# Up-projection of a gated MLP: half of the block moves go from GpSimd to ScalarE, one step behind the transposes, and the silu is issued behind the next evacuation

## The chip, the cores and the metric

The kernel runs on one core of one Trainium2 chip. The metric is the device time of one execution in microseconds. Five engines of the core work side by side, each through its own list of instructions in order: TensorE (PE in the profile; its weight loads are PEld), VectorE (DVE), ScalarE (ACT), GpSimd (POOL) and SyncE (SP), which here issues the loads of the weights. They wait for one another only through semaphores. Before the change three runs took 2243.81 to 2244.72 us, with a median of 2244.45 us.

## The reference

The program is a two-layer encoder over 256 positions of width 2048, in float32. Each layer has attention and then a gated MLP; the change lies in the MLP, which is, cut to what matters (D_FF is 5632):

```python
def conv_ffn(h, w_up, conv_w, conv_b, w_down):
    u = h @ w_up                                  # 256 x 11264: gates, then values
    u = lax.conv_general_dilated(u, conv_w[:, None, :], window_strides=(1,), padding=((1, 1),),
                                 feature_group_count=c) + conv_b   # width 3, along the positions
    gate, val = jnp.split(u, 2, axis=-1)
    return (jax.nn.silu(gate) * val) @ w_down
```

The convolution runs along the positions, channel by channel, so the kernel needs the channels on the partitions after the up-projection, which delivers positions on the partitions. Hence transposes stand between the two.

## The kernel before

**Products.** Every weight arrives as float32 in tiles `raw` of 128x1024 (512 KB). ScalarE rounds such a tile to `wh` (line 144) and VectorE takes the rest, `wl = raw - wh` (line 145). Each weight tile then feeds three passes of TensorE, `xh*wh`, `xh*wl` and `xl*wh` (lines 132 to 134), for two halves of the positions and two rows of weight blocks: twelve products of 128x512. There are four buffers each of `wh` and `wl` (`NHL`), so ScalarE can round a tile only when TensorE has finished with the one four before. In pairs 2, 4, 6 and 8 (`UP`) one of the four quarters of the inner dimension is done in Strassen's way (`fast_unit`, lines 179 and 180), where seven weight tiles feed six products each, and sums of weights and of results go over VectorE.

**The stages of the MLP.** The 5632 channels are 11 pairs of blocks of 512, a gate block and a value block each, in two halves (`HALVES`: pairs 0 to 5, then 6 to 10); after each half the down-projection runs over what is finished. In the profile the up-projections lie at about 290 to 550 and 670 to 850 us (layer 0) and 1550 to 1800 and 1905 to 2150 us (layer 1).

**A block behind the product.** For a gate (`gate_gen`) and a value (`value_gen`):

- ScalarE evacuates two accumulators to `stg` and applies the row scale (`evac_scaled`, line 489, two instructions).
- `turned` lets VectorE transpose 32x32 blocks into `quad` (line 377, two instructions), and then 16 moves of 32 partitions x 256 elements put the blocks in place in `u`. All 16 are GpSimd's (line 562), except for the value of the last pair of a half, where every second one is ScalarE's (line 564).
- `conv` runs the middle tap and the bias on ScalarE (line 541, four instructions) and the two outer taps on VectorE (line 549, eight instructions), into `cg` for a gate and `cv` for a value.
- The gate gets its silu on ScalarE (line 571), in the generator of the next pair's gate; `product` multiplies it with the value on VectorE (line 579); `act_split` or `combined` splits the result for the down-projection.

There are three `u` buffers, used in turn, two `quad`, one `cg` and one `cv`.

**What sets the order.** The generators are advanced by `step`, once for some products of the main line: every `yield` puts what follows one step later in the program. A scheduler then orders each engine's list by priority and dependence; the splits to `wh` and `wl` are pulled 60 places ahead (`tc.high_priority(offset=AHEAD)`), and `tc.issue_after(x)` keeps an instruction behind `x`. What stands in an engine's list is executed in that order, so an instruction that waits holds up all those behind it on its engine.

Of the kernel before, what the change touches and what calls it, by code (L numbers as in the profile page):

```python
# [10 lines left out]
AF = mybir.ActivationFunctionType  # L11
# [14 lines left out]
UP = 2, 4, 6, 8  # L26
UP_ORDER = (1, 0), (2, 0), (3, 0), (0, None), (1, 1), (2, 1), (3, 1)
NWARM = 11
QC = [(q, c) for q in range(4) for c in range(4)]
# [4 lines left out]
def tile_encoder(ctx: ExitStack, tc: tile.TileContext, x, xT, w_a, w_ao, q_gain, k_gain, w_b, w_bo,  # L34
                 rel_bias, gains, w_up, conv, w_down, final_norm, rope, ident_c, onehot, out):
    nc = tc.nc
# [23 lines left out]
    def nm(s):  # L60
        uid[0] += 1
        return f"{s}_{uid[0]}"
# [43 lines left out]
            return pool.tile([P, 2, 512], F32, tag=tags[0], name=nm("raw"), bufs=2 if len(tags) == 1 else 1)  # L106
        return spool.tile([P, 2, 512], F32, tag="raw", name=nm("raw"), bufs=NRAW)

    newest = [None]

    def of_m(x, m):
        return x[m] if isinstance(x, tuple) else x[:, m * P:(m + 1) * P]
# [41 lines left out]
    def new_acc():  # L154
        return [accp.tile([P, 512], F32, tag="acc", name=nm("acc")) for _ in range(2)]
# [214 lines left out]
    def quad_tile(pool, tag, bufs=1):  # L370
        return pool.tile([P, 4, 8, 32], F32, tag=tag, name=nm("quad"), bufs=bufs)
# [4 lines left out]
    def quad_T(quad, at, src):  # L376
        nc.vector.transpose(quad[:, :, at, :], src.rearrange("p (x c t) -> p c x t", c=4, t=32))  # L377
# [73 lines left out]
    def finish_rstd(ss):  # L451
        tot = small.tile([P, 2], F32, tag="tot", name=nm("tot"))
        nc.vector.tensor_reduce(tot, ss, axis=AX.X, op=ALU.add)
        rstd = small.tile([P, 2], F32, tag="rstd", name=nm("rstd"))
        rsqrt_mean(rstd, tot, D)
        return rstd
# [29 lines left out]
    def evac_scaled(pool, accs, rstd, bufs=2):  # L486
        o = pool.tile([P, 2, 512], F32, tag="stg", name=nm("stg"), bufs=bufs)
        for m in range(2):
            nc.scalar.activation(o[:, m, :], accs[m], AF.Copy, scale=rstd[:, m:m + 1])  # L489
        return o  # L490

    def ffn(l, hT, ss_in, cw, g_next, last, side=None):
        with tc.tile_pool(name=nm("fpool"), bufs=1) as fp:
# [7 lines left out]
            rstd = finish_rstd(ss_in)  # L501
# [4 lines left out]
            def fin(c0, c1):  # L506
                return fins[c0 // 512][:, c0 % 512:(c1 - 1) % 512 + 1]
# [43 lines left out]
                    if j == 1:  # L551
                        yield

            def turned(s, u, by_act=False):
                quad = quad_tile(fp, "quad", 2)
                for m in range(2):
                    quad_T(quad, slice(m, 8, 2), s[:, m])
                for i, (q, c) in enumerate(QC):
                    o = u[32 * c:32 * c + 32, :, :, 32 * q:32 * q + 32]
                    src = quad[32 * q:32 * q + 32, c].rearrange("p (j m) t -> p j m t", m=2)  # L560
                    if i % 2 == 0 or not by_act:
                        nc.gpsimd.tensor_copy(o, src)  # L562
                    else:
                        nc.scalar.activation(o, src, AF.Copy)

            def gate_gen(accs, blk, value):
                s = evac_scaled(fp, accs, rstd, 1)
                yield
                turned(s, blk[1])
                if value is not None:  # L570
                    nc.scalar.activation(value[3], value[3], AF.Silu)
                    for _ in range(4 if blk[0] in UP else 2 if blk[0] == 1 else 1):
                        yield
                    yield from product(value)

            def product(value):
                n, u, cv, cg, _, _ = value
                yield from conv((n, u, cv))
                nc.vector.tensor_tensor(cv, cg, cv, ALU.mult)

            def value_gen(accs, blk, gate, last):
                s = evac_scaled(fp, accs, rstd, 1)
                yield
                if gate[0] + 1 in (p for _, p in HALVES):
                    turned(s, blk[1], True)
                    yield
                    yield from conv(gate)
                    nc.scalar.activation(gate[2], gate[2], AF.Silu)
                    yield
                    yield from act_split(last)  # L590
                    return
                turned(s, blk[1])
                wait = 4 if gate[0] in UP else 5 if last is None else 2
                if last is not None:
                    yield
                    for _ in act_split(last):
                        yield
                        wait -= 1
                    wait -= 1
                for _ in range(max(wait, 1)):  # L600
                    yield
                yield from conv(gate)
# [53 lines left out]
            def next_u():  # L656
                us.append(us.pop(0))
                return us[0]
# [70 lines left out]
            for hf, (p0, p1) in enumerate(HALVES):  # L729
# [5 lines left out]
                for p in range(p0, p1):  # L735
# [3 lines left out]
                    gate, value = (p, next_u(), cg), (NPAIR + p, next_u(), cv, cg, slots, k0)  # L739
# [56 lines left out]
                def put(m, c0, c1, how, r):  # L796
                    hs = h[:, m, c0:c1]
                    if how == "fin":
                        nc.vector.scalar_tensor_tensor(hs, hs, r, fin(c0, c1), ALU.mult, ALU.mult)
                    elif how == "act":  # L800
                        nc.scalar.activation(hs, hs, AF.Copy, scale=r)
                    else:
                        nc.vector.tensor_scalar(hs, hs, r, None, op0=ALU.mult)
# [52 lines left out]
                accs = new_acc()  # L856
# [684 lines left out]
```

## Time and profile before

| | |
|---|---|
| median of three runs | 2244.45 us |
| the profiled execution, its own time | 2244.87 us |
| its span, from the first to the last instruction | 2243.1 us |
| mean granted TensorE clock | 0.999 |
| TensorE busy | 2218.4 us (99% of the span) |
| VectorE busy | 1885.2 us (84%) |
| ScalarE busy | 1344.4 us (60%) |
| GpSimd busy | 762.8 us (34%) |

The table of the costliest groups has one row for each line, engine and shape, with the total, the mean of one instruction in ns, the idle time of the engine just before them and what ended it. Its rows on matmuls read 390 ns for one, but they start every 0.227 us: consecutive matmuls overlap. So a time for TensorE has to be read from the starts, in the timeline, or from its idle stretches, in the view of the waits. A wait in that view reads "engine, line that waited <- engine and line that ended the wait: us in total, times, longest".

### The profile page before, as it was taken

Reading aid. Unit: us, or ns where it says so; the run is one execution under the profiler, and the core shown is the slowest. Engines: PE = TensorE matmul, PEld = TensorE weight load, DVE = VectorE, ACT = ScalarE, POOL = GpSimd, SP = SyncE. Lnnn points to the kernel's source line nnn. Section 1 sums busy time; section 2 is a strip of 40 time slices with the busy share of each in tenths; the row PEclk is TensorE's granted clock in tenths of the full one; section 3 lists DMA queues with packets and bytes.
Section 4 is the critical chain, followed back from the end, with each engine's and each line's share of the span. In section 5 each row is a group of like instructions: output and inputs, shape, how many; then the busy total and the mean of one; then the engine's idle time right before and its main releaser. Section 6 shows DMA issues by size and latency. Waiting matters only on the chain.

```text
span 2243.1 us, 28885 instructions
## 1 busy us (share of the span) xinstructions
PE 2218.4 (99%) x9957; PEld 1833.9 (82%) x9957; DVE 1885.2 (84%) x2385; ACT 1344.4 (60%) x1894; POOL 762.8 (34%) x1017
## 2 busy tenths in 40 slices
PE   9999999999999999999999999999999999999998
PEld 7888888788888878888888888888887888887887
DVE  6877678998898998868886878588899898989887
ACT  7666655666455666665454556566666655556664
POOL 2343254753006462040053006003645600255611
PEclk9999999999999999999999999999999999999999
DMA  8575655556656566666656555656556565656654
GB/s 302 192 215 182 218 186 194 183 192 196 203 183 226 175 198 202 197 188 197 188 186 197 179 189 181 195 185 214 174 197 201 185 203 191 215 162 205 226 196 142
DMA packets 126179, 439.59 MB, mean 196 GB/s; under 512 B 14408, under 2 KB 18248, under 8 KB 126032
## 3 DMA queue, kind: packets, MB, share of 16 engines
q1 hardware_dynamic: 123056, 429.05, 58.8%
q0 software_dynamic: 2688, 8.39, 1.5%
q8 instruction: 78, 1.28, 0.2%
q14 instruction: 69, 0.57, 0.1%
q10 hardware_dynamic: 288, 0.30, 0.0%
HBM read 432.34 MB, written 5.34 MB: 195 GB/s over the span
## 4 chain that ended last, share of the span: by engine, by line
PE 42%; DVE 8%; issue 2%; DMA 2%; POOL 1%; ACT 1%; DVEq 0%; POOLq 0%; ACTq 0%
PE acc L133 12%; PE acc L132 12%; PE acc L134 12%; DVE wl L145 3%; DVE wl L180 1%; DVE cv L549 1%; PE ps L187 1%; PE ps L188 1%; PE ps L186 1%; DMA raw<-in_w_b_dram 1%; POOL u L562 1%; DMA raw<-in_w_up_dram 1%; ACT wh L144 1%; DMA raw<-in_w_down_dram 1%; DVE cg L549 1%
## 5 line engine op out<-in xcount | busy, mean ns | idle before, releaser
L145 DVE TENSOR_TENSOR wl<-raw,wh 128x1024 fp32r<-128x1024 f32 (+1 forms) x716 | 898.8, 1266 | 224.2 <-ACT wh L144 218.3
L144 ACT ACTIVATE wh<-raw 128x1024 fp32r<-128x1024 f32 (+1 forms) x716 | 746.0, 1048 | 516.2 <-PE acc L134 391.9
L133 PE MATMUL acc<-wl,xh 128*128 128x512 f32 x2048 | 801.1, 391 | 8.7 <-DVE wl L145 8.7
L132 PE MATMUL acc<-wh,xh 128*128 128x512 f32 x2048 | 800.3, 391 | 1.3 <-ACT wh L144 1.3
L134 PE MATMUL acc<-wh,xh 128*128 128x512 f32 x2048 | 798.3, 390 | 0.0
L562 POOL COPY u<-quad 32x256 f32<-32x256 f32 x672 | 518.3, 771 | 451.1 <-DVE quad L377 414.1
L133 PEld LDWEIGHTS acc<-wl,xh 128*128 128x128 f32 x2048 | 385.2, 188 | 94.6 <-DVE wl L145 17.0
L132 PEld LDWEIGHTS acc<-wh,xh 128*128 128x128 f32 x2048 | 385.2, 188 | 80.8 <-ACT wh L144 2.4
L134 PEld LDWEIGHTS acc<-wh,xh 128*128 128x128 f32 x2048 | 385.0, 188 | 79.4
L132 PE MATMUL acc<-wh,a 128*128 128x512 f32 x720 | 281.1, 390 | 0.0
L133 PE MATMUL acc<-wl,a 128*128 128x512 f32 x720 | 280.7, 390 | 0.0
L134 PE MATMUL acc<-wh,a 128*128 128x512 f32 x720 | 280.3, 389 | 0.0
L179 ACT ACTIVATE wh<-raw 128x1024 fp32r<-128x1024 f32 x112 | 118.7, 1061 | 107.9 <-PE acc L134 82.9
L134 PEld LDWEIGHTS acc<-wh,a 128*128 128x128 f32 x720 | 135.2, 188 | 28.2 <-DVE a L328 0.2
L133 PEld LDWEIGHTS acc<-wl,a 128*128 128x128 f32 x720 | 135.3, 188 | 28.0 <-DVE wl L145 0.6
L132 PEld LDWEIGHTS acc<-wh,a 128*128 128x128 f32 x720 | 135.3, 188 | 27.5
L381 POOL COPY wide<-quad 32x256 f32<-32x256 f32 x133 | 89.3, 672 | 169.3 <-DVE quad L377 159.8
L180 DVE TENSOR_TENSOR wl<-raw,wh 128x1024 fp32r<-128x1024 f32 x112 | 137.2, 1250 | 1.6 <-ACT wh L179 1.0
L398 POOL COPY wide<-quad 32x256 f32<-32x256 f32 x88 | 53.2, 605 | 235.4 <-DVE quad L377 168.3
L489 ACT ACTIVATE stg<-acc,rstd 128x512 f32<-128x512 f32 x122 | 81.5, 682 | 33.5 <-PE acc L134 17.0
L549 DVE SCALAR_TENSOR_TENSOR cg<-u,cw,cg 128x256 f32<-128x256 f32 x176 | 94.3, 581 | 3.4 <-ACT cg L541 3.3
L549 DVE SCALAR_TENSOR_TENSOR cv<-u,cw,cv 128x256 f32<-128x256 f32 x176 | 85.8, 524 | 2.5 <-ACT cv L541 1.9
(310 smaller groups left out, 2198.6 us busy)
## 6 DMA issues: line engine op xcount, KB each, us to landing
raw<-in_w_up_dram SPq DMA_DIRECT2D x352, 512.0 KB, 4.5
raw<-in_w_down_dram SPq DMA_DIRECT2D x176, 512.0 KB, 4.6
raw<-in_w_b_dram SPq DMA_DIRECT2D x144, 512.0 KB, 4.5
raw<-in_w_bo_dram SPq DMA_DIRECT2D x48, 512.0 KB, 4.4
raw<-in_w_a_dram SPq DMA_DIRECT2D x40, 512.0 KB, 4.8
raw<-in_w_ao_dram SPq DMA_DIRECT2D x32, 512.0 KB, 4.6
raw<-in_w_a_dram SPq DMA_DIRECT2D x16, 256.0 KB, 5.8
there<-quad POOLq DMA_DIRECT2D x6, 512.0 KB, 3.7
```

The source lines that it names most:

```text
L132: nc.tensor.matmul(accs[m], xh, wh[:, j, :], start=st, stop=False)
L133: nc.tensor.matmul(accs[m], xh, wl[:, j, :], start=False, stop=False)
L134: nc.tensor.matmul(accs[m], xl, wh[:, j, :], start=False, stop=sp)
L144: nc.scalar.activation(wh[:, c], r[:, c], AF.Copy)
L145: newest[0] = nc.vector.tensor_tensor(wl[:, c], r[:, c], wh[:, c].bitcast(F32), ALU.subtract)
L179: nc.scalar.activation(wh, r, AF.Copy)
L180: nc.vector.tensor_tensor(wl, r, wh.bitcast(F32), ALU.subtract)
L381: nc.gpsimd.tensor_copy(o[32 * c:32 * c + 32, :, 32 * q:32 * q + 32], quad[32 * q:32 * q + 32, c])
L398: nc.gpsimd.tensor_copy(dst, src)
L489: nc.scalar.activation(o[:, m, :], accs[m], AF.Copy, scale=rstd[:, m:m + 1])
L549: nc.vector.scalar_tensor_tensor(cj, halves(flat[:, j, o:o + NT])[:, ::-1], tap(n, j, i), cj, ALU.mult, ALU.add)
L562: nc.gpsimd.tensor_copy(o, src)
```

## The change

`turned` becomes a generator. GpSimd makes the moves with even numbers, for every gate and every value. Then, unless `at_once` is set, it yields, and ScalarE makes the eight others one step later. The value of the last pair of a half passes `at_once` and is as before. The silu is put behind the newest evacuation (`evac[0]`). Some counts of steps are one smaller, since `turned` now takes a step itself.

```diff
-    newest = [None]
+    newest, evac = [None], [None]
...
-            nc.scalar.activation(o[:, m, :], accs[m], AF.Copy, scale=rstd[:, m:m + 1])
+            evac[0] = nc.scalar.activation(o[:, m, :], accs[m], AF.Copy, scale=rstd[:, m:m + 1])
...
-            def turned(s, u, by_act=False):
+            def turned(s, u, at_once=False):
                 quad = quad_tile(fp, "quad", 2)
                 for m in range(2):
                     quad_T(quad, slice(m, 8, 2), s[:, m])
-                for i, (q, c) in enumerate(QC):
-                    o = u[32 * c:32 * c + 32, :, :, 32 * q:32 * q + 32]
-                    src = quad[32 * q:32 * q + 32, c].rearrange("p (j m) t -> p j m t", m=2)
-                    if i % 2 == 0 or not by_act:
-                        nc.gpsimd.tensor_copy(o, src)
-                    else:
-                        nc.scalar.activation(o, src, AF.Copy)
+
+                def move(i, put):
+                    q, c = QC[i]
+                    put(u[32 * c:32 * c + 32, :, :, 32 * q:32 * q + 32],
+                        quad[32 * q:32 * q + 32, c].rearrange("p (j m) t -> p j m t", m=2))
+
+                for i in range(0, 16, 2):
+                    move(i, nc.gpsimd.tensor_copy)
+                if not at_once:
+                    yield
+                for i in range(1, 16, 2):
+                    move(i, partial(nc.scalar.activation, func=AF.Copy))
...
-                turned(s, blk[1])
+                yield from turned(s, blk[1])
                 if value is not None:
-                    nc.scalar.activation(value[3], value[3], AF.Silu)
-                    for _ in range(4 if blk[0] in UP else 2 if blk[0] == 1 else 1):
+                    with tc.issue_after(evac[0].ins):
+                        nc.scalar.activation(value[3], value[3], AF.Silu)
+                    for _ in range(3 if blk[0] in UP else 1):
                         yield
                     yield from product(value)
...
                 if gate[0] + 1 in (p for _, p in HALVES):
-                    turned(s, blk[1], True)
+                    yield from turned(s, blk[1], True)
...
-                turned(s, blk[1])
+                yield from turned(s, blk[1])
                 wait = 4 if gate[0] in UP else 5 if last is None else 2
                 if last is not None:
-                    yield
                     for _ in act_split(last):
```

The lists of TensorE and SyncE hold the same instructions in the same order as before; GpSimd's list has 320 moves fewer, ScalarE's 320 more; VectorE's has the same instructions, some in another order. Line 562 becomes 561, the silu's line 571 becomes 577, and other lines below move by five or six.

The first place is ScalarE's list in pair 2 of layer 0, after the evacuation of that pair's value. `cg<-u` is the middle tap of the pair's gate, `s` and `sx` are splits of the value of the pair before, `u_2635` is where this value's blocks go. Before:

```order
L489 ACTIVATE stg_3770<-acc_3362,rstd_2629 128x512
L144 ACTIVATE wh_3891<-raw_3887 128x1024
L541 ACTIVATE cg_3357<-u_2637,cw_555 128x256 x2
L144 ACTIVATE wh_3909<-raw_3889 128x1024
L541 ACTIVATE cg_3357<-u_2637,cw_555 128x256 x2
L320 ACTIVATE s_3842<-st_3837 128x1024
L320 ACTIVATE sx_3844<-cv_2994 128x512
L320 ACTIVATE sx_3844<-cv_2994 128x256
L144 ACTIVATE wh_3935<-raw_3931 128x1024
```

Now:

```order
L489 ACTIVATE stg_3770<-acc_3362,rstd_2629 128x512
L144 ACTIVATE wh_3891<-raw_3887 128x1024
L541 ACTIVATE cg_3357<-u_2637,cw_555 128x256 x2
L561 ACTIVATE u_2635<-quad_3802 32x8x32 x2
L144 ACTIVATE wh_3909<-raw_3889 128x1024
L561 ACTIVATE u_2635<-quad_3802 32x8x32 x6
L144 ACTIVATE wh_3935<-raw_3931 128x1024
L320 ACTIVATE s_3842<-st_3837 128x1024
L320 ACTIVATE sx_3844<-cv_2994 128x512
L320 ACTIVATE sx_3844<-cv_2994 128x256
L144 ACTIVATE wh_3955<-raw_3933 128x1024
L541 ACTIVATE cg_3357<-u_2637,cw_555 128x256 x2
```

Eight moves came in around `wh_3909`, and `wh_3935` now stands ahead of the three splits and of two of the four taps.

The second place is VectorE's list in pair 8 of layer 0, ahead of and behind `wl_7168`. `cv_6325` is the value of the pair before, first under its outer taps, then multiplied with its gate; the two rows on `acc` are the last sums of this pair's result. Before:

```order
L145 TENSOR_TENSOR wl_7131<-raw_7088,wh_7130 128x1024
L549 SCALAR_TENSOR_TENSOR cv_6325<-u_5965,cw_555,cv_6325 128x256 x3
L579 TENSOR_TENSOR cv_6325<-cg_6324,cv_6325 128x1024
L723 TENSOR_TENSOR acc_6692<-acc_6692,fold_6930 128x512
L724 TENSOR_TENSOR acc_6693<-acc_6693,fold_6930 128x512
L145 TENSOR_TENSOR wl_7168<-raw_7163,wh_7167 128x1024
L145 TENSOR_TENSOR wl_7184<-raw_7165,wh_7183 128x1024
L377 STREAM_TRANSPOSE quad_7111<-stg_7079 128x16x32 x2
```

Now:

```order
L145 TENSOR_TENSOR wl_7123<-raw_7088,wh_7122 128x1024
L549 SCALAR_TENSOR_TENSOR cv_6325<-u_5965,cw_555,cv_6325 128x256 x3
L145 TENSOR_TENSOR wl_7168<-raw_7163,wh_7167 128x1024
L728 TENSOR_TENSOR acc_6692<-acc_6692,fold_6930 128x512
L729 TENSOR_TENSOR acc_6693<-acc_6693,fold_6930 128x512
L549 SCALAR_TENSOR_TENSOR cv_6325<-u_5965,cw_555,cv_6325 128x256
L145 TENSOR_TENSOR wl_7184<-raw_7165,wh_7183 128x1024
L585 TENSOR_TENSOR cv_6325<-cg_6324,cv_6325 128x1024
L377 STREAM_TRANSPOSE quad_7111<-stg_7079 128x16x32 x2
```

`wl_7168` has moved ahead of the product and the two sums.

The third place is ScalarE's list in pair 8 of layer 0, behind the evacuation of its value, where the silu of its gate `cg_6688` stands. Before it was followed by the taps of the value, with `wh` in between:

```order
L144 ACTIVATE wh_7328<-raw_7290 128x1024
L571 ACTIVATE cg_6688<-cg_6688 128x1024
L541 ACTIVATE cv_6689<-u_5964,cw_555 128x256 x2
L144 ACTIVATE wh_7350<-raw_7346 128x1024
L541 ACTIVATE cv_6689<-u_5964,cw_555 128x256 x2
L489 ACTIVATE stg_7283<-acc_7084,rstd_2629 128x512
L489 ACTIVATE stg_7283<-acc_7085,rstd_2629 128x512
L144 ACTIVATE wh_7372<-raw_7348 128x1024
```

Now:

```order
L541 ACTIVATE cv_6689<-u_5964,cw_555 128x256 x2
L489 ACTIVATE stg_7283<-acc_7084,rstd_2629 128x512
L489 ACTIVATE stg_7283<-acc_7085,rstd_2629 128x512
L144 ACTIVATE wh_7366<-raw_7346 128x1024
L577 ACTIVATE cg_6688<-cg_6688 128x1024
L561 ACTIVATE u_5965<-quad_7308 32x8x32
L144 ACTIVATE wh_7392<-raw_7388 128x1024
L561 ACTIVATE u_5965<-quad_7308 32x8x32 x6
L144 ACTIVATE wh_7413<-raw_7390 128x1024
L561 ACTIVATE u_5965<-quad_7308 32x8x32
L541 ACTIVATE cv_6689<-u_5964,cw_555 128x256 x2
```

The silu moved behind the evacuation of the next gate (`stg_7283`), and that gate's moves stand right behind it.

## The prediction, made before the result was seen

> **What bounds the kernel now.** I read the busy times first, then the windows of the four up-projection stretches, then TensorE's own waits there, and last the timeline around the longest of them. The busy times, and the windows of those stretches (columns: length, then busy time and count of PE, PEld, DVE, ACT and POOL):
>
> ```profile
> PE 2218.4 (99%) x9957; PEld 1833.9 (82%) x9957; DVE 1885.2 (84%) x2385; ACT 1344.4 (60%) x1894; POOL 762.8 (34%) x1017
> ...
> 290.00:550.00 260.00, 256.45 (x1128) 210.96 (x1128) 234.69 (x286) 162.16 (x213) 145.77 (x185) 1.00 0.59 190
> 670.00:850.00 180.00, 178.20 (x782) 146.10 (x781) 162.10 (x197) 109.66 (x138) 102.82 (x132) 1.00 0.62 202
> 1550.00:1800.00 250.00, 248.15 (x1090) 203.66 (x1089) 226.91 (x277) 158.17 (x206) 141.07 (x184) 1.00 0.59 193
> 1905.00:2150.00 245.00, 242.94 (x1067) 199.45 (x1066) 218.49 (x267) 149.02 (x192) 118.05 (x156) 1.00 0.61 200
> sum 935.00, PE 925.74 PEld 760.16 DVE 842.18 ACT 579.01 POOL 507.70; mean PE 231.43 PEld 190.04 DVE 210.55 ACT 144.75 POOL 126.93
> ```
>
> TensorE bounds it, at full clock (the 1.00). Its products are untouched, so what can be won is only its stalls in these stretches: 935.0 - 925.7 = 9.3 us of idle time. VectorE stands next at 842/935 = 90%, ScalarE at 62%, GpSimd at 54%. TensorE's waits in the whole program, and one stall start by start (columns: start, us, instruction, idle before it):
>
> ```profile
> PE acc L133 <- DVE wl L145: 8.7, 11, 2.3
> PE ps L187 <- DVE wl L180: 2.0, 2, 1.2
> PE acc L132 <- ACT wh L144: 1.3, 2, 0.8
> ...
> 796.33 0.39 PE L134 MATMUL acc<-wh,xh 128*128 128x512 f32 x1
> 796.56 0.39 PE L132 MATMUL acc<-wh,xh 128*128 128x512 f32 x1
> 798.23 0.50 PE L133 MATMUL acc<-wl,xh 128*128 128x512 f32 x1 [1.29 <-DVE wl L145]
> 798.57 0.39 PE L134 MATMUL acc<-wh,xh 128*128 128x512 f32 x1
> ...
> 999.73 0.39 PE L134 MATMUL acc<-wh,xh 128*128 128x512 f32 x1
> 1007.89 0.39 PE L134 MATMUL acc<-wh,xh 128*128 128x512 f32 x1
> ```
>
> It almost always waits for `wl`, so for VectorE, seldom for `wh`. Between the last two rows lie 36 starts without a stall: 8.16/36 = 0.227 us each. Here the gaps are 1.67 and 0.34: 1.44 + 0.11 = 1.55 us lost for 1.29 of idle time, so 0.26 more for each stall. The stalls in the stretches are about nine (9.3 us at about 1 us each): 9.3 + 9 x 0.26 = 11.7 us is all that this change can recover there.
>
> **What makes VectorE late, and what half the moves buy.**
>
> ```profile
> L562 POOL COPY u<-quad 32x256 f32<-32x256 f32 x672 | 518.3, 771 | 451.1 <-DVE quad L377 414.1
> L549 DVE SCALAR_TENSOR_TENSOR cg<-u,cw,cg 128x256 f32<-128x256 f32 x176 | 94.3, 581 | 3.4 <-ACT cg L541 3.3
> L549 DVE SCALAR_TENSOR_TENSOR cv<-u,cw,cv 128x256 f32<-128x256 f32 x176 | 85.8, 524 | 2.5 <-ACT cv L541 1.9
> ...
> L549 DVE SCALAR_TENSOR_TENSOR cg<-u,cw,cg x176: 443/611/617, 310.5 to 2132.6; 128x256 f32<-128x256 f32 x176
> ...
> L145 DVE TENSOR_TENSOR wl<-raw,wh 128x1024 fp32r<-128x1024 f32 x38 | 46.5, 1223 | 7.8 <-ACT wh L144 7.2
> ...
> L145 DVE TENSOR_TENSOR wl<-raw,wh 128x1024 fp32r<-128x1024 f32 x4 | 5.4, 1355 | 0.0
> L723 DVE TENSOR_TENSOR acc<-acc,fold 128x512 f32<-128x512 f32 x1 | 0.7, 680 | 0.0
> ...
> L145 DVE TENSOR_TENSOR wl<-raw,wh 128x1024 fp32r<-128x1024 f32 x82 | 106.1, 1307 | 21.9 <-ACT wh L144 21.9
> L145 DVE TENSOR_TENSOR wl<-raw,wh 128x1024 fp32r<-128x1024 f32 x59 | 77.3, 1325 | 16.9 <-ACT wh L144 16.8
> L145 DVE TENSOR_TENSOR wl<-raw,wh 128x1024 fp32r<-128x1024 f32 x81 | 106.0, 1324 | 19.8 <-ACT wh L144 19.7
> L145 DVE TENSOR_TENSOR wl<-raw,wh 128x1024 fp32r<-128x1024 f32 x81 | 104.7, 1306 | 24.0 <-ACT wh L144 23.8
> ...
> L562 POOL COPY u<-quad x672: 391/480/2955, 298.8 to 2135.5; 32x256 f32<-32x256 f32 x168
> ```
>
> The first `wl` row is from a stretch of attention (1234 to 1342 us) without GpSimd work, the second from 786 to 798 us, where GpSimd moves blocks without a break; the last four are the up-projections of the two halves of layer 0 and of layer 1; rows with three numbers give min/median/max of one. With moves beside it an outer tap takes 0.611 instead of 0.443 us and a `wl` 1.355 instead of 1.223, while the sum that reads an accumulator takes 0.68. Over all taps that is 94.3 + 85.8 - 352 x 0.443 = 24.2 us; the 303 `wl` of the stretches took 394.1 - 303 x 1.223 = 23.5 us too long. 320 of 672 moves leave GpSimd, 48%: about 0.48 x 48 = 23 us of VectorE's time come back, 2.5% of the stretches. That the moves left on GpSimd get faster too is not counted.
>
> The Trainium skill explains these rows (SBUF — State Buffer, "Who interferes with whom"): a VectorE instruction with two SBUF inputs and a GpSimd instruction that reads SBUF exclude each other on a shared port for a whole instruction, and ScalarE never waits. The trace agrees in kind (two-input taps and `wl` stretch, 0.611 and 1.355 us, the accumulator sum does not), but not in a full exclusion of each other. Taken at its word each of the 320 moves would have held the port for its undisturbed 0.39 us (the shortest in the last row), an estimated 125 us in place of my 23, all stalls would go, and the sum would be 2233.2 us.
>
> **What it costs ScalarE.** 22 pairs with a gate and a value are 44 groups of moves; 4 are divided already, so 40 x 8 = 320 moves go over. The same move in its ScalarE form, and eight of them in a row between two `wh`:
>
> ```profile
> L564 ACT ACTIVATE u<-quad 32x256 f32<-32x256 f32 x32 | 13.4, 420 | 0.8 <-DVE quad L377 0.4
> ...
> 525.03 1.05 ACT L144 ACTIVATE wh<-raw 128x1024 fp32r<-128x1024 f32 x1
> 526.28 3.44 ACT L564 ACTIVATE u<-quad 32x256 f32<-32x256 f32 x8 [0.20 <-DVE quad L377]
> 529.75 1.06 ACT L144 ACTIVATE wh<-raw 128x1024 fp32r<-128x1024 f32 x1
> ```
>
> 320 x 0.42 = 134 us, so ScalarE rises from 579 to 713 of 935 us (76%), inside its 356 us of idle time. Queued behind the moves is the next `wh`, for which VectorE's `wl` and then TensorE wait. Four `wh` buffers hold 4 x 12 products x 0.227 = 10.9 us; less the next `wh` (1.06) and `wl` (1.36), ScalarE may be away some 8.5 us from full buffers. Eight moves take 3.44. Alone, they cost nothing; where other lateness is added, up to the third rival below. I take 1.5 us in all, between 0 (a bound given by the stretch above, where TensorE did not stall) and that rival's price.
>
> The silu's move buys room:
>
> ```profile
> ACT cg L571 <- DVE cg L549: 47.9, 18, 5.7
> ...
> 801.20 1.06 ACT L571 ACTIVATE cg<-cg 128x1024 f32<-128x1024 f32 x1 [5.44 <-DVE cg L549]
> ```
>
> ScalarE stood 47.9 us at 18 silus, up to 5.7 at a time, with evacuations and `wh` behind it. Two or three instructions later most of this is covered by the evacuation and a `wh`. The product on VectorE waits for the silu; in the order it has moved back as well. The DMA issues of SyncE stand unchanged; GpSimd's issue of `scr<-ln` stands behind eight moves instead of sixteen, so it comes earlier.
>
> **The stalls one by one.** The longest, in pair 2 of layer 0, is GpSimd's own:
>
> ```profile
> 381.17 18.20 POOL L562 COPY u<-quad 32x256 f32<-32x256 f32 x16 [19.28 <-DVE quad L377]
> ...
> 399.40 1.10 ACT L541 ACTIVATE cg<-u,cw 128x256 f32<-128x256 f32 x2 [4.29 <-POOL u L562]
> ...
> 406.26 0.49 PE L132 MATMUL acc<-wh,xh 128*128 128x512 f32 x1 [0.43 <-ACT wh L144]
> 409.01 0.50 PE L133 MATMUL acc<-wl,xh 128*128 128x512 f32 x1 [2.25 <-DVE wl L145]
> ```
>
> Sixteen moves ended at 399.37; ScalarE stood 4.29 us for them with `wh` queued behind, and TensorE ran dry. With eight they end by 390.3 even at this pace, ScalarE's eight take 3.4, and in the new list (first place shown) `wh_3935` stands ahead of three splits and two taps. This stall goes: 0.43 + 2.25 + 2 x 0.26 = 3.2 us. The stall at 783.05 us is for `wl_7168` (second place): ahead of it a product and two sums (0.68 each) are gone; the product, and the wait:
>
> ```profile
> 779.37 1.30 DVE L579 TENSOR_TENSOR cv<-cg,cv 128x1024 f32<-128x1024 f32 x1
> ...
> 783.05 0.50 PE L133 MATMUL acc<-wl,xh 128*128 128x512 f32 x1 [0.52 <-DVE wl L145]
> ```
>
> 1.3 + 2 x 0.68 = 2.7 us against a wait of 0.52 us: 0.52 + 0.26 = 0.8 us back. The stall at 798.23 is VectorE busy from 786 on with nothing but stretched instructions; four `wl` at 0.13 and some ten smaller ones at 0.17 are 2.2 us too long, half of it 1.1, against 1.29: most of its 1.55 goes. The rest, 11.7 - 5.6 = 6.1 us, is the like in other pairs and in layer 1. If every stall went, 11.7 us; I take 70%, since 2.5% of VectorE's time is freed evenly and the stalls sit where it is latest: 8.2.
>
> Sum: 2244.87 - 8.2 + 1.5 = 2238.2 us against the profiled execution. That stands 0.42 above the median, so against the median 2237.8; I say **2238.0 us**.
>
> **The rivals.**
>
> *Freed where nobody waits* (about no change). VectorE's time comes back in stretches where TensorE has buffers, and where it is late the order decides. For it: most of 303 `wl` are in time already, and the tail of the stalls comes from sums in the fast units, which no move touches. Against it: the two longest stalls stand beside moves. Only the stall by GpSimd goes (3.2), less 1.5: 2242.7 us.
>
> *ScalarE is late* (slower). Its list is in order, and now silu and eight moves can follow each other (third place): a wait for VectorE's taps as before (5.44), silu 1.06 and moves 3.4 are 9.9 us against the 8.5 that the buffers allow, 1.4 us of stall. In the eight pairs with a fast unit, where the waits are long, that is 11 us; half of the recovery, 6, stays: 2244.45 + 5 = 2249.5 us. It decides from a wait of about 4 us ahead of the silu or the moves on. Against it: the silu now stands later, so its taps are older, and `wh` stands between the moves in that list.
>
> *All stalls go* and ScalarE costs nothing: 2244.45 - 11.7 = 2232.8 us, the skill's reading above among its grounds.
>
> **How the numbers follow.** The forecast, with its own range of 2234.5 to 2240.5, has 0.48, all stalls gone 0.10, freed where nobody waits 0.25, ScalarE late 0.17. A measurement tells 0.2% (4.5 us) from no change, so faster begins below 2240.0. Of the forecast 0.45 lies there and all of the fourth, so faster 0.55; the second and the remainder make no change 0.29; slower, above 2248.9, has 0.16. The range reaches 2232 below, the bound of all stalls, and 2248.5 above.
>
> **What would show it.** GpSimd's row with 352 moves, nearer to 0.6 than 0.77 us each; ScalarE's with 352 at 0.42; taps nearer to 0.50 and `wl` in the stretches nearer to 1.26; TensorE's idle time in the stretches at 3 to 4 us instead of 9.3; no wait of the middle taps for GpSimd; the 47.9 us ahead of the silu at half or less. It is wrong if TensorE waits for `wl` as long as before, or if "PE <- ACT wh" grows: that is ScalarE late, and then VectorE's wait for `wh` in the stretches grows with it.

## The result and the profile after

| | before | after |
|---|---|---|
| median of six runs | 2243.69 us | 2235.26 us |
| lowest and highest | 2241.04 to 2244.72 us | 2234.22 to 2235.73 us |
| span of the profiled execution | 2243.1 us | 2233.6 us |

The ratio after to before is 0.9963 with a 95% interval of 0.995 to 0.9976: 8.4 us faster. The forecast was 2238.0 us, with a range of 2232.0 to 2248.5. The direction came out, and so did the mechanism of the gain; the two terms of the sum were both too small, in opposite directions, and the second acts by another path than the one forecast, as the experiments will show.

First the engines' busy times of the changed kernel, and then the sum over the four up-projection stretches that were read of before (their length, then the busy time of each engine; the granted clock is 1.00 in all four):

```profile
PE 2215.7 (99%) x9957; PEld 1832.7 (82%) x9957; DVE 1832.3 (82%) x2385; ACT 1477.5 (66%) x2214; POOL 482.6 (22%) x697
```

```profile
sum 935.00, PE 931.72 PEld 766.94 DVE 792.93 ACT 715.40 POOL 235.84; mean PE 232.93 PEld 191.73 DVE 198.23 ACT 178.85 POOL 58.96
```

TensorE's idle time in the stretches fell from 9.3 to 935.0 - 931.7 = 3.3 us. By the starts of the products (every gap beyond the pitch of 0.227 us added up) it lost 13.5 us there before and 6.5 now. That is 7.0 of the 9.5 us by which the span shrank; 1.5 more were won in the first down-projection of layer 1, which follows the third stretch, and 0.8 lies ahead of the first up-projection, in work that the change does not touch.

VectorE's work in the whole program fell by 1885.2 - 1832.3 = 52.9 us, ScalarE's rose by 133.1 us and GpSimd's fell by 280.2 us. The groups that changed (total, mean of one in ns, idle time before them and what ended it):

```profile
L561 POOL COPY u<-quad 32x256 f32<-32x256 f32 x352 | 236.3, 671 | 710.8 <-DVE quad L377 692.8
L561 ACT ACTIVATE u<-quad 32x256 f32<-32x256 f32 x352 | 147.9, 420 | 10.4 <-DVE quad L377 5.4
L549 DVE SCALAR_TENSOR_TENSOR cv<-u,cw,cv 128x256 f32<-128x256 f32 x176 | 81.1, 504 | 0.0
L549 DVE SCALAR_TENSOR_TENSOR cg<-u,cw,cg 128x256 f32<-128x256 f32 x176 | 78.9, 490 | 0.8 <-ACT cg L541 0.5
...
L145 DVE TENSOR_TENSOR wl<-raw,wh 128x1024 fp32r<-128x1024 f32 x82 | 102.2, 1256 | 30.2 <-ACT wh L144 30.2
L145 DVE TENSOR_TENSOR wl<-raw,wh 128x1024 fp32r<-128x1024 f32 x60 | 74.8, 1259 | 26.4 <-ACT wh L144 26.3
L145 DVE TENSOR_TENSOR wl<-raw,wh 128x1024 fp32r<-128x1024 f32 x81 | 101.2, 1260 | 28.3 <-ACT wh L144 28.3
L145 DVE TENSOR_TENSOR wl<-raw,wh 128x1024 fp32r<-128x1024 f32 x81 | 101.5, 1265 | 34.4 <-ACT wh L144 34.4
```

The outer taps went from 581 and 524 to 490 and 504 ns, the `wl` of the four up-projections from 1306 to 1325 down to 1256 to 1265 ns. But look at the last column: VectorE now stands 30.2 + 26.3 + 28.3 + 34.4 = 119.2 us in front of these `wl` until ScalarE has rounded `wh`; before it was 82.2. That is 37 us more, but not all of it comes from ScalarE's new work: in a kernel that leaves the eight moves out and adds nothing to ScalarE (half_moves, below) the same sum is 105.5 us. A VectorE that is done earlier waits longer for `wh`. The same wait in the whole program, before, in half_moves and now:

```profile
DVE wl L145 <- ACT wh L144: 218.3, 197, 4.3
```

```profile
DVE wl L145 <- ACT wh L144: 238.0, 208, 4.6
```

```profile
DVE wl L145 <- ACT wh L144: 249.9, 224, 3.9
```

TensorE's waits in the whole program:

```profile
PE ps L187 <- DVE wl L180: 2.6, 6, 0.5
PE acc L133 <- DVE wl L145: 2.6, 7, 1.0
```

The wait for `wl` of line 145 fell from 8.7 to 2.6 us. All three stalls that the prediction went through one by one (near 406 and 409, 783 and 798 us) are gone, and so are their counterparts in layer 1. In the fast units the waits moved. The first row above was 2.0 us in two places before and is 2.6 in six now, one in each of six of the eight pairs with a fast unit; another wait for line 180, in the down-projections and below as it was before, has fallen to 0.3 us in one place:

```profile
PE acc L187 <- DVE wl L180: 1.4, 4, 0.5
```

By the starts of the products these six places cost more than the waits say: 1.0 to 1.25 us each, 6.5 us in all, which is everything that TensorE still loses in the stretches. The kernel before lost 3.0 us there, nearly all of it in two of the six. VectorE's timeline in the first of them (start, duration) shows why:

```profile
356.48 1.22 DVE L180 TENSOR_TENSOR wl<-raw,wh 128x1024 fp32r<-128x1024 f32 x1
357.62 0.48 DVE L549 SCALAR_TENSOR_TENSOR cg<-u,cw,cg 128x256 f32<-128x256 f32 x1
358.02 1.22 DVE L178 TENSOR_TENSOR raw<-raw,raw 128x1024 f32<-128x1024 f32 x1
359.15 1.22 DVE L180 TENSOR_TENSOR wl<-raw,wh 128x1024 fp32r<-128x1024 f32 x1
360.29 1.22 DVE L178 TENSOR_TENSOR raw<-raw,raw 128x1024 f32<-128x1024 f32 x1
361.42 0.48 DVE L549 SCALAR_TENSOR_TENSOR cg<-u,cw,cg 128x256 f32<-128x256 f32 x1
```

Taps of the gate, which come later now, stand between the fast unit's own sums and splits: three in each of the six, and VectorE does not stand still between the unit's first split and its last. Before, one tap stood ahead of the unit, and the run behind it was line 178 and line 180 alone.

### The profile page after: what moved, and what is told of

Its sections match the earlier page's. It is cut to its first block, busy times and chain, and to the rows that moved or that the text cites. A ratio compares the mean times of both kernels' runs of the same rounds, so it can differ in the third digit from the quotient of the medians.

```text
span 2233.6 us, 28902 instructions
## 1 busy us (share of the span) xinstructions
PE 2215.7 (99%) x9957; PEld 1832.7 (82%) x9957; DVE 1832.3 (82%) x2385; ACT 1477.5 (66%) x2214; POOL 482.6 (22%) x697
## 4 chain that ended last, share of the span: by engine, by line
PE 50%; DVE 4%; issue 1%; DMA 1%; POOL 1%; ACT 1%; POOLq 0%; DVEq 0%; ACTq 0%
PE acc L133 15%; PE acc L134 15%; PE acc L132 15%; DVE wl L180 1%; DVE wl L145 1%; PE ps L188 1%; PE ps L187 1%; PE ps L186 1%; DVE raw L178 1%; DMA raw<-in_w_b_dram 1%; PE acc L187 1%; PE acc L188 1%; PE acc L186 1%; DVE tT L386 0%; ACT wh L144 0%
## 5 line engine op out<-in xcount | busy, mean ns | idle before, releaser
L145 DVE TENSOR_TENSOR wl<-raw,wh 128x1024 fp32r<-128x1024 f32 (+1 forms) x716 | 880.4, 1239 | 256.0 <-ACT wh L144 249.9
L561 POOL COPY u<-quad 32x256 f32<-32x256 f32 x352 | 236.3, 671 | 710.8 <-DVE quad L377 692.8
L561 ACT ACTIVATE u<-quad 32x256 f32<-32x256 f32 x352 | 147.9, 420 | 10.4 <-DVE quad L377 5.4
L549 DVE SCALAR_TENSOR_TENSOR cv<-u,cw,cv 128x256 f32<-128x256 f32 x176 | 81.1, 504 | 0.0
```

The lines of the kernel that those rows point to most:

```text
L145: newest[0] = nc.vector.tensor_tensor(wl[:, c], r[:, c], wh[:, c].bitcast(F32), ALU.subtract)
L549: nc.vector.scalar_tensor_tensor(cj, halves(flat[:, j, o:o + NT])[:, ::-1], tap(n, j, i), cj, ALU.mult, ALU.add)
L561: put(u[32 * c:32 * c + 32, :, :, 32 * q:32 * q + 32], quad[32 * q:32 * q + 32, c].rearrange("p (j m) t -> p j m t", m=2))
```

## The experiments

The open questions: which part of the change carries the gain, whether it comes through GpSimd's reading beside VectorE or through the shorter chain of moves, and what ScalarE's new work costs. Each diff is against the changed kernel unless another is named; each ratio is to the kernel before, measured on the same chip.

### The moves without the silu's new place (moves_only)

```diff
-                    with tc.issue_after(evac[0].ins):
-                        nc.scalar.activation(value[3], value[3], AF.Silu)
+                    nc.scalar.activation(value[3], value[3], AF.Silu)
```

> The change without the hold on the silu: ScalarE makes every second move one step later, the silu stands where it stood. Three theories. Port: GpSimd's moves slow VectorE's two-input instructions, and fewer of them give VectorE time back. Chain: sixteen moves in a row on one engine finish late, and what waits for them (middle taps, and wh behind them) is late. Silu: the gain is ScalarE no longer standing ahead of the silu. Port and chain: most of the 8.4 us stays, 2235 to 2238 us, with the wait ahead of the silu at 30 us or more. Silu: 2240 us or more.

2235.09 us, 0.9972 (0.9961 to 0.9982): within the interval of the whole change. Its row for the silu:

```profile
L576 ACT ACTIVATE cg<-cg 128x1024 f32<-128x1024 f32 x18 | 19.1, 1061 | 22.9 <-DVE cg L549 22.9
```

ScalarE stands 22.9 us ahead of the 18 silus here; 47.9 before, nothing with the whole change. Half of the wait had gone with the moves alone, and removing the rest bought nothing that these runs can tell.

### The silu's new place without the moves (silu_only)

The kernel before with `evac[0]` and `issue_after`; all 16 moves stay on GpSimd.

```diff
-                    nc.scalar.activation(value[3], value[3], AF.Silu)
+                    with tc.issue_after(evac[0].ins):
+                        nc.scalar.activation(value[3], value[3], AF.Silu)
```

> The kernel before with nothing but the hold on the silu behind the newest evacuation; GpSimd makes all the moves. Port and chain: 2242 to 2245 us, no change that can be measured, taps still at 0.52 to 0.58 us, and the stall of 2.25 us in pair 2 of layer 0 stays. Silu: 2236 to 2239 us.

2241.31 us, 0.9996 (0.9987 to 1.0005): no change. TensorE's timeline has the old long stall where it was, and the middle taps wait for GpSimd longer than before, 12.9 + 5.5 = 18.4 us in these two rows instead of 10.7, which stood ahead of the gate's alone (idle time before them on the right; the last row is of the kernel before):

```profile
408.14 0.80 PE L133 MATMUL acc<-wl,xh 128*128 128x512 f32 x1 [2.25 <-DVE wl L145]
```

```profile
L541 ACT ACTIVATE cv<-u,cw 128x256 f32<-128x256 f32 x88 | 47.6, 588 | 12.9 <-POOL u L562 12.9
L541 ACT ACTIVATE cg<-u,cw 128x256 f32<-128x256 f32 x88 | 47.3, 590 | 5.5 <-POOL u L562 5.5
```

```profile
L541 ACT ACTIVATE cg<-u,cw 128x256 f32<-128x256 f32 x88 | 47.3, 590 | 10.7 <-POOL u L562 10.7
```

So the 47.9 us in front of the silu were no room: part of the wait moved to the next instruction that needed GpSimd. The moves carry the gain.

### GpSimd's reading put back, and a clean pair (gpsimd_reads, gpsimd_writes, reads_again, writes_again)

The first pair added eight instructions on GpSimd to each group of moves: casts of the same blocks to a scratch tile, or memsets of that tile.

```diff
+                for i in range(0 if at_once else 8):
+                    q, c = QC[2 * i + 1]
+                    nc.gpsimd.tensor_copy(spare_t[32 * c:32 * c + 32],
+                                          quad[32 * q:32 * q + 32, c, :6].rearrange("p (j m) t -> p j m t", m=2))
```

> The changed kernel, and GpSimd makes eight further copies behind its eight moves, from the same quad buffer into a scratch tile that nobody reads (192 of the 256 elements each). Nothing waits for them, so the chain of moves is as short as in the change, but GpSimd reads SBUF about as long as before the change. Port: VectorE is slowed again (taps 0.55 us or more, wl in the up-projections 1.29 or more) and at least half of the gain is lost: 2239 us or more. Chain and silu: within 2 us of the changed kernel.

> As the run with the further copies, in the same order on every engine, but the eight are memsets of the scratch tile: GpSimd writes SBUF and reads nothing. Port through the reads: VectorE is not slowed (taps 0.50, wl 1.26) and the time is that of the changed kernel, 2234 to 2237 us. If any work of GpSimd slows VectorE: as with the copies. Chain and silu: the time of the changed kernel here and with the copies.

The casts: 2252.93 us, 1.0054 (1.0041 to 1.0066). The memsets, which should have been harmless: 2258.05 us, 1.0081 (1.0067 to 1.0095). The time of the second says nothing about ports. A memset into scratch depends on nothing, and the scheduler put 156 of them in a row; then ScalarE waits for the real moves behind them (timeline), and TensorE 9.1 us for ScalarE:

```profile
1540.69 47.56 POOL L569 MEMSET sparet<- 32x192 bf16 x156
...
1591.79 1.09 ACT L542 ACTIVATE cg<-u,cw 128x256 f32<-128x256 f32 x2 [16.20 <-POOL u L562]
```

The rows of the pair do point to reading: a tap of the gate takes 526 ns beside the casts and 497 beside the memsets. But the lists differ, so the pair was made again with instructions tied to the moves: after GpSimd's eight, it copies the same eight blocks of `quad` onto themselves, or clears them. The lists of TensorE, VectorE and ScalarE are identical in the two kernels.

```diff
+                for q, c in QC[:0 if at_once else 16:2]:
+                    b = quad[32 * q:32 * q + 32, c].rearrange("p (j m) t -> p j m t", m=2)
+                    nc.gpsimd.tensor_copy(b, b)         # reads_again
+                    nc.gpsimd.memset(b, 0.0)            # writes_again
```

> The changed kernel, and behind its eight moves GpSimd copies the eight blocks that it has just moved onto themselves, in quad (32x256, as long as a move). Nobody waits for these copies before the buffer's next turn. TensorE, VectorE and ScalarE have the same lists as in the run with memsets, so the two differ in GpSimd's instruction alone. Port: GpSimd reads SBUF as long as before the change, taps 0.54 us or more and wl in the up-projections 1.29 or more, and the time is at least 4 us above the run with memsets. Chain: the moves that anyone waits for are as early as in the change, so both runs agree within 2 us.

> The same with memsets of these eight blocks, which now cannot start ahead of their moves. GpSimd writes and reads nothing. Port through the reads: taps 0.49 to 0.51 us, wl 1.26, and 2234 to 2239 us, the order of VectorE's list differing a little from the change's. If any work of GpSimd slows VectorE: as with the copies.

2257.55 us, 1.0062 (1.005 to 1.0075), against 2239.95 us, 0.999 (0.9981 to 0.9999). First the groups and TensorE's waits of the kernel that reads:

```profile
L568 POOL COPY quad<-quad 32x256 f32<-32x256 f32 x320 | 227.8, 737 | 9.1
L549 DVE SCALAR_TENSOR_TENSOR cg<-u,cw,cg 128x256 f32<-128x256 f32 x176 | 88.9, 546 | 0.7 <-ACT cg L541 0.5
L145 DVE TENSOR_TENSOR wl<-raw,wh 128x1024 fp32r<-128x1024 f32 x82 | 105.5, 1301 | 24.0 <-ACT wh L144 24.0
```

```profile
PE acc L133 <- DVE wl L145: 11.2, 12, 2.9
PE ps L187 <- DVE wl L180: 7.2, 12, 1.0
```

Then the same of the kernel that only writes:

```profile
L568 POOL MEMSET quad<- 32x256 f32 x320 | 89.2, 305 | 8.6
L549 DVE SCALAR_TENSOR_TENSOR cg<-u,cw,cg 128x256 f32<-128x256 f32 x176 | 78.5, 488 | 0.7 <-ACT cg L541 0.5
L145 DVE TENSOR_TENSOR wl<-raw,wh 128x1024 fp32r<-128x1024 f32 x81 | 100.9, 1257 | 28.6 <-ACT wh L144 28.6
```

```profile
PE acc L133 <- DVE wl L145: 5.1, 10, 1.5
```

The same number of instructions at the same places: where they read, a tap of the gate takes 546 ns, a `wl` 1301, and 17.6 us are lost; where they only write, 488 and 1257, as in the changed kernel with no extra instruction. One thing still differs, the length of the extra ones (737 against 305 ns), so GpSimd is free sooner in the second kernel; but none of the largest waits of VectorE and ScalarE in either is for GpSimd's moves. What VectorE suffered from was reading on GpSimd.

A part of the 17.6 us comes at second hand. Behind the two longest gaps between products of the kernel that reads, 3.31 and 3.39 us, TensorE's granted clock is 0.5 for 3.4 us. One of these stretches (length, busy times, clock in the third column from the end), and starts of products in it:

```profile
801.00:804.40 3.40, 3.20 (x8) 2.56 (x9) 3.40 (x6) 0.08 (x1) 0.40 (x1) 0.50 0.53 164
```

```profile
803.49 0.63 PE L132 MATMUL acc<-wh,xh 128*128 128x512 f32 x1
803.92 0.63 PE L133 MATMUL acc<-wl,xh 128*128 128x512 f32 x1
```

The products start every 0.43 us instead of 0.227, which loses 1.6 us each time, 3.2 in all. The kernel that only writes has no such stretch in its up-projections.

writes_again is some 5 us slower than the change itself (6 by the ratios), although its taps and `wl` are as fast. Eight more instructions per group shift what lies 60 places ahead, and some 45 rows of VectorE's list stand elsewhere: that is about the size of what order alone does here.

### Both halves of the moves in one step (no_step)

```diff
                 for i in range(0, 16, 2):
                     move(i, nc.gpsimd.tensor_copy)
-                if not at_once:
-                    yield
                 for i in range(1, 16, 2):
                     move(i, partial(nc.scalar.activation, func=AF.Copy))
+                if not at_once:
+                    yield
```

> The changed kernel with ScalarE's eight moves in the same step as the transposes and GpSimd's eight, and the yield behind them. If the step between matters (ScalarE would stand for the transposes with wh behind): the wait of ScalarE's moves for the transposes grows from 5 to 20 us or more, and 2238 us or more. If the scheduler's order makes up for it: 2234 to 2237 us.

2237.47 us, 0.9981 (0.9972 to 0.999), which overlaps the change's interval. ScalarE's moves do not wait longer for the transposes:

```profile
L561 ACT ACTIVATE u<-quad 32x256 f32<-32x256 f32 x352 | 147.8, 420 | 9.8 <-DVE quad L377 4.9
```

9.8 us against 10.4 with the step: the scheduler fills the time with other work either way. By the medians the step is worth 2 us, by the ratios 4, and these runs do not tell that from nothing.

### How many on ScalarE: four or all (four_scalar, all_scalar)

```diff
+                for i in range(1, 16, 4):
+                    move(i, partial(nc.scalar.activation, func=AF.Copy) if at_once else nc.gpsimd.tensor_copy)
...
-                for i in range(1, 16, 2):
+                for i in range(3, 16, 4):
```

```diff
-                    move(i, nc.gpsimd.tensor_copy)
+                    move(i, nc.gpsimd.tensor_copy if at_once else partial(nc.scalar.activation, func=AF.Copy))
```

> The changed kernel with four moves of each 16 on ScalarE, one step late, and twelve on GpSimd. Relief and load both half: 2237 to 2239.5 us, half the gain. If the relief comes with the first moves and the load later: 2235 us or less, and then fewer moves on ScalarE would be the better kernel.

> The changed kernel with all 16 moves on ScalarE except for the last value of each half; GpSimd's moves go from 352 to 32. Port: VectorE gains as much again, taps 0.45 us, wl 1.23. ScalarE's busy time in the up-projections rises by 134 to about 850 of 935 us. If ScalarE has the room: 2230 to 2234 us. If it becomes the late engine: TensorE waits for wh, 2240 us or more. I expect the latter.

Four of 16: 2239.3 us, 0.9991 (0.9982 to 1.0). All 16: 2295.34 us, 1.0235 (1.0221 to 1.0249). With almost no reading on GpSimd VectorE is at its fastest (the group of the first up-projection, below), and yet the kernel is slowest, and here TensorE waits for `wh` too:

```profile
L145 DVE TENSOR_TENSOR wl<-raw,wh 128x1024 fp32r<-128x1024 f32 x78 | 93.8, 1219 | 49.7 <-ACT wh L144 49.7
```

```profile
PE acc L132 <- ACT wh L144: 15.2, 6, 3.4
PE acc L133 <- DVE wl L145: 13.4, 21, 1.3
```

```profile
402.06 6.88 ACT L561 ACTIVATE u<-quad 32x256 f32<-32x256 f32 x16
...
411.85 0.73 PE L132 MATMUL acc<-wh,xh 128*128 128x512 f32 x2 [2.98 <-ACT wh L144]
```

Sixteen moves in a row keep ScalarE from rounding for 6.88 us, and 2.98 us of TensorE's time are lost behind them, at a busy share of ScalarE of 766/935 = 82% in the stretches. Shortly behind this stall, too, the granted clock is 0.5 for 3.4 us.

### ScalarE's load with and without GpSimd's relief (scalar_extra, half_moves)

The first gives GpSimd all 16 moves back and lets ScalarE copy the eight odd blocks for nothing, one step later; the scratch is bf16 with 192 of 256 elements. The second leaves ScalarE's eight moves out (`u` is cleared once per half instead, so half of its blocks stay zero).

```diff
-                for i in range(0, 16, 2):
+                for i in range(0, 16, 2 if at_once else 1):
                     move(i, nc.gpsimd.tensor_copy)
...
+                    for q, c in QC[1::2]:
+                        nc.scalar.activation(spare_t[32 * c:32 * c + 32],
+                                             quad[32 * q:32 * q + 32, c, :6].rearrange("p (j m) t -> p j m t", m=2),
+                                             AF.Copy)
```

```diff
-                    nc.gpsimd.memset(u[:, :, 0, P:], 0.0)
+                    nc.gpsimd.memset(u, 0.0)
...
                 if not at_once:
                     yield
+                    return
```

> The changed kernel, but GpSimd makes all 16 moves again, and in the place of its eight moves ScalarE copies the same eight blocks (192 of 256 elements) to a scratch tile that nobody reads. VectorE is slowed by GpSimd as before the change, and ScalarE has the change's load. Net of two large terms (what the run with copies on GpSimd suggests: VectorE's relief about -18 us, ScalarE's load about +10): 2250 us or more. ScalarE's load nearly free, as predicted (+1.5 us): within 2 us of the run with the silu alone moved, 2240 to 2244 us.

> Leaves out work: GpSimd's eight moves of each 16 are made and ScalarE's eight are left out (the u buffers are cleared once for each half; the last value of each half is as in the change). So GpSimd reads as little as in the change and ScalarE has the load of before: the fourth corner beside before (much, low), the run with ScalarE's further copies (much, high) and the change (little, high). If ScalarE's load costs the same 16 us at little reading, it falls by as much as TensorE's stalls in the up-projections allow, some 5 us, to about 2230 us. If the load costs only beside GpSimd's reads: within 2 us of the change, 2233.5 to 2237 us.

2258.16 us, 1.0071 (1.0058 to 1.0083), and 2228.64 us, 0.9934 (0.992 to 0.9947). With silu_only and the change itself they make a table of ratios to the kernel before:

| | ScalarE without the eight | ScalarE with them |
|---|---|---|
| GpSimd reads 16 blocks | 0.9996 (silu_only) | 1.0071 (scalar_extra) |
| GpSimd reads 8 blocks | 0.9934 (half_moves) | 0.9963 (the change) |

Down the left column, GpSimd's relief is worth 0.62%, 14 us. Along the lower row, ScalarE's eight moves cost 0.29%, 6.5 us; along the upper, beside much reading, 0.75% or 17 us; down the right column the relief is worth 1.08%, 24 us. The change goes from the upper left to the lower right: -14 + 6.5. The lists of the four kernels are not identical, so each of these carries an uncertainty of the size of the order's effect above, some 5 us.

The stretches of half_moves, which has nearly nothing left to stall for in the up-projections:

```profile
sum 935.00, PE 934.64 PEld 773.40 DVE 817.69 ACT 586.68 POOL 253.52; mean PE 233.66 PEld 193.35 DVE 204.42 ACT 146.67 POOL 63.38
```

VectorE is busier there than in the changed kernel, 817.7 against 792.9 us, and TensorE stands idle for 0.4 us instead of 3.3. So it is not the amount of VectorE's own work that makes `wl` late in the changed kernel. TensorE's list is the same in both, so the starts can be compared product by product: the six fast units lose 6.5 us with the change and nothing in half_moves. In the first of them half_moves has the gate's taps behind it when the splits begin, and VectorE has time to wait for ScalarE:

```profile
355.45 0.47 DVE L549 SCALAR_TENSOR_TENSOR cg<-u,cw,cg 128x256 f32<-128x256 f32 x1
355.84 1.21 DVE L180 TENSOR_TENSOR wl<-raw,wh 128x1024 fp32r<-128x1024 f32 x1
357.09 2.48 DVE L178 TENSOR_TENSOR raw<-raw,raw 128x1024 f32<-128x1024 f32 x2
...
361.01 1.23 DVE L180 TENSOR_TENSOR wl<-raw,wh 128x1024 fp32r<-128x1024 f32 x1 [0.30 <-ACT wh L179]
```

In the changed kernel ScalarE is not late with `wh` at this place either; it stands for a full buffer:

```profile
361.81 1.06 ACT L179 ACTIVATE wh<-raw 128x1024 fp32r<-128x1024 f32 x1 [1.70 <-PE acc L134]
```

What comes later is the gate's middle tap, which stands in ScalarE's list behind the eight moves: from 353.24 us here, from 347.85 in half_moves. VectorE's outer taps follow it and fall between the splits. What is lost goes with the order: no_step, with the same eight moves on ScalarE, has one tap in each of the six units instead of three and loses 2.9 us there. The step alone does not bring the taps in, since half_moves keeps it. Beside much reading it is the same place again, 14.4 us in the six units of scalar_extra against 1.3 in silu_only, of the 17 us between them.

How far ScalarE is ahead of TensorE can be read off another wait, how long it stands because all `wh` buffers are full. The row of the changed kernel, of half_moves and of all_scalar:

```profile
ACT wh L144 <- PE acc L134: 333.2, 237, 2.4
```

```profile
ACT wh L144 <- PE acc L134: 434.7, 303, 2.4
```

```profile
ACT wh L144 <- PE acc L134: 250.3, 176, 2.4
```

It falls with ScalarE's load, but it does not order the times: moves_only has 318.1 us and reads_again 337.6, at 2235.09 and 2257.55 us.

### A longer lead for the splits (ahead68)

```diff
-AHEAD = 60
+AHEAD = 68
```

> The changed kernel with the splits pulled 68 instead of 60 places ahead, everywhere. In the change TensorE waits 0.4 to 0.5 us in each of six fast units for a wl that stands behind a tap of the gate in VectorE's list (some 3 us in all). If the order of VectorE's list makes these: fewer of them, 2231 to 2234 us. The number acts on the whole program, so it can lose elsewhere: 2238 us or more would say that the list was better as it is.

2233.69 us, 0.9961 (0.9947 to 0.9975): not to be told from the change. The six fast units still have two or three taps of the gate in them and lose less, 3.6 us by the starts instead of 6.5, but the sum of stalls in the stretches is 6.6 us as against 6.5: what was won there was lost elsewhere. Eight places more for everything do not give the time back.

## Why the prediction was right, and where it was off

**What bounds the kernel.** Right: TensorE stayed at 99%, and what was won lies in its stalls in the up-projections. They were put at 11.7 us; by the starts they were 13.5.

**VectorE is slowed by GpSimd's reading.** Right, and shown by the pair with identical lists: 17.6 us between reading and writing. About 23 us of VectorE's time were to come back; about 50 did. The step "that the moves left on GpSimd get faster too is not counted" hid part of it (they went from 771 to 671 ns, so they overlap less), and the count took only taps and `wl` of line 145: of 52.9 us they are 20.1 and 14.4, the remainder lies in other work of VectorE. The number of moves does not settle it alone: with the same 352 moves on GpSimd, half_moves got 842.2 - 817.7 = 24.5 us back in the stretches, and its taps still take 521 and 537 ns.

**"If every stall went, 11.7 us; I take 70%": 8.2.** Too small as a price of the relief. half_moves has the relief without ScalarE's moves, and its stalls in the stretches are 0.9 instead of 13.5 us: 93% of them go. The three stalls gone through singly behaved as said.

**"Alone, they cost nothing [...] I take 1.5 us in all" for ScalarE's moves.** This is the term that was sized worst, 6.5 us beside little reading, and its path was wrong. The working named the next `wh` as what is queued behind the moves. On that path it was right for this load: TensorE hardly ever waits for `wh`, and in the first of the six fast units ScalarE stands for a full buffer. What it passed over is the other thing queued behind the moves, the gate's middle taps, and with them the place of VectorE's outer taps: three of them in each of six fast units, 1.0 to 1.25 us each time. The working on moved instructions went through the places of the old stalls alone. The sign named for the rival *ScalarE is late*, VectorE's longer wait for `wh`, did appear (82.2 to 119.2 us), but half_moves shows 105.5 us without the load, so the sign was not a good one. That rival's mechanism decides at more load, as all_scalar shows; here it did not.

The two errors, relief short by about 6 us and the price of ScalarE's moves short by about 5, cancelled; that the forecast came so near is in part luck. The net of -6.7 us in the sum against the measured -8.4 looked better than its parts.

**"The silu's move buys room."** Wrong: the wait went from 47.9 us to nothing, and neither silu_only nor the comparison of moves_only with the change shows a gain.

**The skill's rule taken at its word** (SBUF — State Buffer, "Who interferes with whom") spoke of exclusion for a whole instruction and led to 2233.2 us, nearer to the result than the forecast, but for another reason: with the reading halved the stalls for which VectorE was late before did nearly all go, and what kept the time up were the gate's taps in the fast units. The same section says that a two-input instruction of VectorE contends with a GpSimd instruction that reads SBUF and not with one that only writes it; the pair of runs agrees, 546 against 488 ns for a tap. A full exclusion these runs do not show.

**Open.** No run holds the gate's taps out of the fast units and leaves all else as it is, so that the 6.5 us would then come back is argued from VectorE's list and TensorE's starts. In no_step and ahead68, which lose less in the six units, other places lost more, and the stretches lost 7.7 and 6.6 us in all. The number of taps is not all of it: four_scalar has one tap in four of the six units, like no_step, and loses 1.0 us in each of them instead of 0.5. How much of the relief is GpSimd's reading and how much its shorter row of moves is not separated either: where the kernel before lost 3.2 us at its first stall, reads_again, which has the reading but the short row, loses 0.8.

## What to carry to other kernels

Where VectorE feeds the bound engine, count what GpSimd reads from SBUF beside VectorE's two-input instructions: a small copy moved elsewhere can pay although it is no cheaper there (420 ns on ScalarE, 391 at best on GpSimd). The engine that takes it over is judged by what stands behind the new work in its list, not by its busy share alone: here going from 62% to 76% cost 6.5 us, lost where the gate's taps came later, 82% made the kernel 53 us slower than before, and eight of 16 was the best of 0, 4, 8 and 16. When a chain gets longer on one engine, look where its last instructions land in the list of the engine that feeds the bound one. A predicted net that comes out right says little of its terms until one kernel has each of them alone, and a dummy instruction put in for that needs a dependence that holds it in place.

## What the runs showed of the hardware

GpSimd's memsets of 32x256 took 305 ns beside VectorE and left its taps (488 ns) and `wl` (1257 ns) where they were; copies of the same size took 737 ns and stretched them to 546 and 1301 ns. GpSimd's copies lose more by the overlap than VectorE's instructions do: its moves take 391 ns at the least and 671 (the change) to 771 (before) on average, a `wl` 1219 with almost no reading on GpSimd and 1306 to 1325 with all 16 moves there. ScalarE's copies of 32x256 took 419 to 421 ns in every kernel, whatever ran beside them. Behind gaps of 3.31 and 3.39 us between products the granted clock was 0.5 for 3.4 us, and products started every 0.43 us instead of 0.227.
